# One layer of a hybrid attention step on one core: a measured cost model for the order of instructions, jobs on the divided array issued together, and a scan at the end of a search

## The chip, the cores and the metric

One NeuronCore of a Trainium2 chip runs the kernel. The time is device microseconds of one execution; the median of three runs is given. One further execution was recorded by the hardware profiler, and its rows are the ones quoted. Engines: PE is TensorE, PEld its weight loads, DVE is VectorE, ACT is ScalarE, POOL is GpSimd, SP issues the DMAs.

## The reference, cut to what matters

One layer step is computed for a prompt of 512 tokens and a sample of 32 tokens, each of width 1024. The sample has caches of 1024 past positions (the newest 512 of them for group A).

```
z = rmsnorm(x) @ w_in          # 1024 x 3880: q, k, v, gate of A, B; q, gate of M; indexer
A: 6 heads x 64, own chunk of 64 and 8 chunks before, learned relative bias
B: 6 heads x 64, rotary; an indexer of 8 heads x 32 gives
   score(q, s) = sum_h w_h relu(qi_h . ki_s);  the k best keys per query are attended
   (k = 128 for the prompt's 512 keys, 256 for the sample's 1024 + 32)
M: 4 heads x 64 over 256 memory tokens, k and v from rmsnorm(mem) @ w_mem_kv
x = x + concat(oA*silu(gA), oB*silu(gB), oM*silu(gM)) @ w_out
y = rmsnorm(x)                 # and the new keys and values are outputs too
```

Top k takes the lower position first among equal scores, which is why the search of the sample's choice has an end for ties.

## The kernel before, in words

All weights come from memory as 32-bit floats. ACT rounds each block to a short form (`wh`), POOL or DVE subtracts to get the rest (`wl`), and the activations are split in the same way (`xTh`, `xTl`, `oAh`, `oAl`). A projection is then three matmuls for each block of 128 inputs: `wh` by `xTh`, `wh` by `xTl`, `wl` by `xTh`. These make up most of PE's work. The projections run in the order of two lists, `EARLY` (A, M) and `LATE` (gate, k, q, v of B); then comes the output projection in chunks of columns, first for A and M (weights times `oA`, `oM`, `oS`), then for B (`oB`). `oS` is the sample's part.

Everything else is a task: a Python generator that issues some instructions and yields a time at which it wants to go on. Such tasks are the indexer (`index`), the prompt's picks with MAX and MATCH_REPLACE on `ysel`, the search of the sample's choice (`sample_choice`), the attention units (`attend`), the sample's attention (`sample`), and the evictions of banks (`evict`). A unit is one pair of heads with one tile of 128 queries or two: score matmuls (`u.begin`, named k,q in the rows), then DVE and ACT make `z` by mask, exp, sum and scaling, PE transposes `z` (ident,z), and `u.mix` multiplies with v (pt,vb). The result `o` is gated on DVE while it leaves its bank.

The order is set while the program is written. The class `Line` keeps a clock for each engine; each recorded instruction advances it by `cost`, and `lag` is what a result needs from one engine to another. The stream of projections is fill: before each of its steps `run` lets all tasks go on whose time has come by the model's clock. So a change of `cost` moves instructions on all engines. All instructions are issued through one helper, `Timed`, which is why every row of the profile names the same line.

PE can be divided with `tile_position`: products with only 64 or 32 rows or columns then run side by side on parts of the array. The sample's raw projection (`raw`, `xF`), scores and mixes of units and the sample's scores and mixes do so. `room` waits for a free bank of the eight.

The sample's choice is a search over bits of a threshold for 256 of 1056 keys for each of the 32 queries, four candidates at a time on 128 partitions. A pass is one Sign of 1056 on ACT with its sum, a Sign of the sum (`bf_ok`), a matmul of one column (bf_ok,over) that counts, and small operations on DVE. Before, a second search of six such passes over `rank` (positions among the equal scores) ended it.

At the end each tile of 128 rows gets its second half of 512 columns from PE; `residual` adds x on DVE, `settle` squares it with a sum on ACT, adds and takes the power on POOL (`ss`), and scales the second half on DVE and the first on ACT before the store.

Of the kernel before, what the change touches and what calls it, by code (L numbers as in the profile page):

```python
# [36 lines left out]
SURE = 1.0  # L37
LAG = 0.2
# [6 lines left out]
class Line:  # L45
# [4 lines left out]
    def __init__(self):  # L50
        self.clk = dict.fromkeys(("PE", "DVE", "ACT", "POOL", "SP", "DMA"), 0.0)
        self.ready, self.used = {}, {}
        self.boxes = {}
        self.tables = {"exp": (AF.Exp, AF.Tanh)}
        self.table = None
        self.tasks = []
        self.seq = 0
        self.margin = 0.3
        self.time = 0.0
        self.window, self.busy, self.slow = 0.0, 0.0, True  # L60
        self.warm = None

    def cost(self, eng, op, outs, ins, kw):
        if eng == "PE":
            w = 1 if ins[0].dtype in (F32R, BF16) else 2 if op == "transpose" else 4
            n = outs[0].free_size() * w / 2400.0
            if op == "matmul" and ins[0].dtype == F32R:
                return 0.003 + max(n, 0.104) if "tile_position" not in kw else 0.02 + 0.5 * max(n, 0.104)
            if "tile_position" in kw:
                return 0.04 + n * (0.25 if outs[0].shape[0] == T else 0.5)  # L70
            return 0.003 + n
        n = max(x.free_size() for x in outs[:1] + ins[:1])
        chip = ins and ins[0].space != PSUM
        if eng == "DVE":
            if op == "tensor_scalar" and chip and outs[0].dtype == F32 and "accum_out" not in kw:
                return 0.13 + n / 1920.0
            return (0.13 if op == "scalar_tensor_tensor" and chip else 0.07) + n / 960.0
        if eng == "ACT":
            t = 0.05 + 0.045 * bool(chip) + n / 1200.0 + (0.19 if "accum_out" in kw else 0)
            for table, fs in self.tables.items():  # L80
                if kw.get("func") in fs and self.table != table:
                    self.table = table
                    t += 1.3
            return t
        return 0.15 + n * (0.0034 if op == "tensor_scalar" else 0.0021)
# [56 lines left out]

    def op(self, eng, op, outs, ins, kw):
# [126 lines left out]
def hybrid_step(ctx: ExitStack, tc: tile.TileContext, a: dict):  # L270
# [37 lines left out]

    def take(k):
# [146 lines left out]
    def w_sample():  # L456
        for nm, i, n in parties:
# [3 lines left out]
            yield from room()  # L461
            p = bank()
            for j in (0, 2):
                for q in range(4):
                    PE.matmul(p[q * T:(q + 1) * T, 0:n], xF[:, 2 * j + q, :], raws[i + j + q // 2][:, q % 2, :],
                              start=(j == 0), stop=(j == 2), tile_position=(0, q * T))
# [3 lines left out]
    def sample_rows(nm, n, p):  # L470
# [15 lines left out]
        yield from line.wait(lambda: NT in normed)  # L486
# [451 lines left out]
    bf = {n: cp.tile([P, 1], F32, name="bf_" + n) for n in ("sum", "t", "c", "m", "need", "cut", "try", "dig", "min")}  # L938
# [3 lines left out]
    def sample_choice():  # L942
        flp, neg, ok, dig, nxt = (bi[n] for n in ("flip", "neg", "ok", "dig", "next"))
        thr = bi["thr0"], bi["thr1"]
        s_, t, c, m, need, cut, tr_, digf, okf = (bf[n] for n in ("sum", "t", "c", "m", "need", "cut", "try", "dig", "ok"))
# [4 lines left out]
        V.tensor_copy(digf, dig)  # L950
# [5 lines left out]
        def passed(of, bias, least_, scale=1.0):  # L956
# [3 lines left out]
            A.activation(okf, s_, AF.Sign, bias=least_, scale=scale)  # L960
# [29 lines left out]
        yield from line.wait(lambda: count["scored"] >= len(TILES))  # L990
# [19 lines left out]
        V.tensor_scalar(need, c, -2.0, float(2 * TOPK_S - NKS) + 0.5, op0=ALU.mult, op1=ALU.add)  # L1010
        G.iota(rank, pattern=[[-1, NKS]], base=2048, channel_multiplier=0, allow_small_or_imprecise_dtypes=True)
        yield max(line.at(rank), line.idle(V))
        V.scalar_tensor_tensor(rank, ysS, t, rank, op0=ALU.is_equal, op1=ALU.mult)
        V.memset(cut, 2048.5)
        V.tensor_scalar(tr_, digf, 1024.0, cut, op0=ALU.mult, op1=ALU.subtract)
        for b in range(10, -1, -2):
            w = float(1 << b)
            p = yield from passed(rank, tr_, need, -1.0)
            V.tensor_scalar(m, p[:, 0:1], 0.5 * w, 1.5 * w, op0=ALU.mult, op1=ALU.add)
            give(p)  # L1020
            V.tensor_scalar(cut, m, -1.0, cut, op0=ALU.mult, op1=ALU.add)
            if b:
                V.tensor_scalar(tr_, digf, 0.25 * w, cut, op0=ALU.mult, op1=ALU.subtract)
# [3 lines left out]
        V.scalar_tensor_tensor(ysS, rank, cut, ysS, op0=ALU.is_le, op1=ALU.mult)  # L1027
# [103 lines left out]
    def sample(mix, nh, nb, kt, cv, qT, kn, vn, pts, zin):  # L1131
# [18 lines left out]
        for g0 in range(0, nh, 4):  # L1150
# [9 lines left out]
            yield from room(len(cuts))  # L1160
            scs = [bank() for _ in cuts]
            for sc, (k0, n) in zip(scs, cuts):
                for j, h in enumerate(hs):
                    r = 64 * (h % 2)
                    PE.matmul(sc[T * j:T * j + T, 0:n], qT[r:r + 64, h // 2, -T:], kt[h // 2][r:r + 64, k0:k0 + n], start=True, stop=True,
                              tile_position=(r, T * j))
# [42 lines left out]
            for j0 in range(0, len(hs), 2):  # L1209
                for pt, b, i, w in blocks:  # L1210
                    for j in (j0, j0 + 1):
                        h = hs[j]
                        e = h % 2
                        vv = cv[b // 4][:, b % 4, h * 64:h * 64 + 64] if b < nb else vn[:, h * 64:h * 64 + 64]
                        PE.matmul(o_ps[64 * e:64 * e + 64, (h // 2) * T:(h // 2 + 1) * T], vv,
                                  pt[:, i * rows + T * j:i * rows + T * j + T], start=(b == 0),
                                  stop=(b * P + w == nk), tile_position=(0, 64 * e))
# [143 lines left out]
    class Masked:  # L1361
# [74 lines left out]
        def mix(self, pts, o):  # L1436
            for i, (t, c, n) in enumerate(self.parts):
                for b in range(n // P):
                    for e in range(2):
# [3 lines left out]
                                  tile_position=(0, 64 * e))  # L1443

# [21 lines left out]
    def attend(i):  # L1466
# [10 lines left out]
        yield from room(2)  # L1477
        sc = u.begin()
# [11 lines left out]
        yield from room()  # L1490
        o = bank()
        u.mix(pts, o)
# [46 lines left out]
    line.until(lambda: 1 in gated and all(n in over for n in ("kb", "qb", "vb")))  # L1539
# [38 lines left out]
    def out_part(parts, c0, n, done, order):  # L1578

        ws = [w_next(1 + i) for i in range(len(parts))]  # L1580
        for t in order:
            acc, = take(1)
            for i, ((m, k0, nk, p0, pn), (wh, wl)) in enumerate(zip(parts, ws)):
                o = acc[:, p0:p0 + pn]
# [15 lines left out]
            line.spawn(evict([acc], [1], lambda _, p, t=t: residual(t, p, c0, n), lambda t=t: done(t)))  # L1600
# [6 lines left out]
    for c0 in range(0, D, 256):  # L1607
        line.run(out_part(((0, 0, 3, 0, 256), (2, 6, 2, 0, 256)), c0, 256, lambda t: None, (0, 1, 2, 3, NT)))
# [10 lines left out]
    def settle(t, c0):  # L1619
        rows = P if t < NT else T  # L1620
        x = xr[t][:, c0:c0 + 512]
        s_ = ss[:rows, t, :]
        last = c0 + 512 == D
        yield line.at(x) - 0.2
        A.activation(sq[:rows], x, AF.Square, scale=D ** -0.5, accum_out=s_[:, c0 // 512:c0 // 512 + 1])
        if not last:
            G.tensor_tensor(x, x, gf[:rows, c0:c0 + 512], op=ALU.mult)
        yield line.at(s_) - 0.2
        if not last:
            V.tensor_scalar(s_[:, 2:3], s_[:, 0:1], EPS, None, op0=ALU.add)  # L1630
            return
        G.tensor_tensor(s_[:, 3:4], s_[:, 1:2], s_[:, 2:3], op=ALU.add)
        G.tensor_tensor(s_[:, 4:5], s_[:, 3:4], nhalf[:rows], op=ALU.pow)
        yield line.at(s_) - 0.2
        y = xr[t]
        V.scalar_tensor_tensor(x, x, s_[:, 4:5], gf[:rows, c0:D], op0=ALU.mult, op1=ALU.mult)
        A.activation(y[:, 0:512], y[:, 0:512], AF.Copy, scale=s_[:, 4:5])
        DMA.dma_start(a["y_prompt"][t * P:(t + 1) * P, :] if t < NT else a["y_sample"], y)

    for c0 in range(0, D, 512):  # L1640
        line.run(out_part(((1, 3, 3, 0, 256), (1, 3, 3, 256, 256)), c0, 512, lambda t, c0=c0: line.spawn(settle(t, c0)),
                          (NT, 0, 1, 2, 3)))
# [67 lines left out]
```

## Time and profile before

| | |
|---|---|
| median of 3 runs | 369.21 us (368.37 to 370.45) |
| profiled execution, its own time | 369.7 us |
| its span in the profile | 367.9 us |
| mean granted clock of PE | 0.992 |
| from the start of the span to the first wait's end on PE | 1.35 us |
| DMA | 46.35 MB, mean 126 GB/s |
| DVE, ACT, POOL busy | 282.4, 223.0, 176.2 us |

The profiled execution's time is 1.8 above its span, for what lies around the profiled instructions. A row of a timeline has start, length, engine, the program's line, operation, output and inputs, shapes and, in brackets, idle time before it with what ended it. Ends of matmuls are modelled and overlap; the distance of two starts is what one costs. Rows of the page's groups have the count, then busy us and mean ns.

### The profile page before, as it was taken

Reading aid. Unit: us, or ns where it says so; the run is one execution under the profiler, and the core shown is the slowest. Engines: PE = TensorE matmul, PEld = TensorE weight load, DVE = VectorE, ACT = ScalarE, POOL = GpSimd, SP = SyncE. Lnnn points to the kernel's source line nnn. Section 1 sums busy time; section 2 is a strip of 40 time slices with the busy share of each in tenths; the row PEclk is TensorE's granted clock in tenths of the full one; section 3 lists DMA queues with packets and bytes.
Section 4 is the critical chain, followed back from the end, with each engine's and each line's share of the span. In section 5 each row is a group of like instructions: output and inputs, shape, how many; then the busy total and the mean of one; then the engine's idle time right before and its main releaser. Section 6 shows DMA issues by size and latency. Waiting matters only on the chain.

```text
span 367.9 us, 7969 instructions
## 1 busy us (share of the span) xinstructions
PE 355.6 (97%) x2959; PEld 321.6 (87%) x2959; DVE 282.4 (77%) x731; ACT 223.0 (61%) x524; POOL 176.2 (48%) x202
## 2 busy tenths in 40 slices
PE   8999999999999999999999998999999999999992
PEld 8989679999989988889899787898999879899991
DVE  2682996989999999999999989986764676623553
ACT  5865756997776946788737343767864556311343
POOL 1787953475443834446548447352145206233651
PEclk9999999999999999999999998999999999999998
DMA  7996631366483330611322115121147932120005
GB/s 252 361 361 220 172 116 43 130 178 172 127 272 104 116 89 11 175 47 45 86 64 67 45 48 172 37 59 54 48 159 259 375 98 88 43 102 2 0 20 224
DMA packets 41478, 46.35 MB, mean 126 GB/s; under 512 B 5184, under 2 KB 36544, under 8 KB 41440
## 3 DMA queue, kind: packets, MB, share of 16 engines
q1 hardware_dynamic: 41440, 45.85, 39.2%
q8 instruction: 23, 0.38, 0.4%
q14 instruction: 15, 0.12, 0.1%
HBM read 39.67 MB, written 6.16 MB: 125 GB/s over the span
## 4 chain that ended last, share of the span: by engine, by line
PE 77%; DVE 11%; ACT 3%; POOL 3%; issue 2%; DMA 2%; SPq 1%; POOLq 0%; ACTq 0%; DVEq 0%
PE bank L240 77%; DMA raw<-in_w_in_dram 2%; DVE rt L240 1%; POOL wl L240 1%; DVE rank L240 1%; DVE KSs L240 1%; ACT sq L240 1%; DVE ysel L240 1%; DVE kb L240 1%; POOL ss L240 1%; DVE kbS L240 1%; DVE m L240 1%; SPq L240 1%; DVE bf_m L240 1%; POOL kb L240 1%
## 5 line engine op out<-in xcount | busy, mean ns | idle before, releaser
L240 POOL TENSOR_TENSOR wl<-raw,wh 128x512 fp32r<-128x512 f32 (+2 forms) x68 | 105.1, 1553 | 95.6 <-ACT wh L240 91.8
L240 PE MATMUL bank<-wh,xTh 128*128 128x384 f32 (+1 forms) x192 | 67.5, 351 | 0.1
L240 ACT ACTIVATE wh<-raw 128x512 fp32r<-128x512 f32 (+2 forms) x70 | 49.8, 717 | 28.4 <-issue 11.8
L240 PE MATMUL bank<-wl,xTh 128*128 128x384 f32 (+1 forms) x192 | 64.0, 334 | 0.2 <-DVE wl L240 0.2
L240 PE MATMUL bank<-wh,xTl 128*128 128x384 f32 (+1 forms) x192 | 63.7, 332 | 0.0
L240 ACT ACTIVATE z<-z,st 128x256 f32<-128x256 f32 (+3 forms) x76 | 40.6, 549 | 35.1 <-DVE st L240 35.0
L240 PE MATMUL bank<-xTh,wh 128*128 128x272 f32 x208 | 46.3, 304 | 0.3 <-DVE stS L240 0.3
L240 PE MATMUL bank<-xTh,wl 128*128 128x272 f32 x208 | 43.0, 288 | 0.0
L240 PE MATMUL bank<-xTl,wh 128*128 128x272 f32 x208 | 43.0, 288 | 0.0
L240 PEld LDWEIGHTS bank<-wh,xTh 128*128 128x128 f32 x192 | 36.6, 191 | 3.9 <-issue 2.6
L240 PEld LDWEIGHTS bank<-wl,xTh 128*128 128x128 f32 x192 | 36.5, 190 | 0.6 <-DVE wl L240 0.4
L240 PEld LDWEIGHTS bank<-wh,xTl 128*128 128x128 f32 x192 | 36.8, 191 | 0.3 <-DVE xTl L240 0.3
L240 PEld LDWEIGHTS bank<-xTh,wh 128*128 128x128 f32 x208 | 32.7, 189 | 3.1 <-issue 2.0
L240 PEld LDWEIGHTS bank<-xTl,wh 128*128 128x128 f32 x208 | 32.6, 188 | 0.0
L240 PEld LDWEIGHTS bank<-xTh,wl 128*128 128x128 f32 x208 | 32.5, 189 | 0.0
L240 DVE MAX8 m<-ysel 128x8 f32<-128x256 f32 (+2 forms) x48 | 26.4, 550 | 0.1
L240 DVE MATCH_REPLACE8 ysel<-m,ysel 128x256 f32<-128x256 f32 (+2 forms) x48 | 26.0, 542 | 0.0
L240 PE MATMUL bank<-ident,z 128*128 128x128 f32 (+1 forms) x161 | 25.2, 274 | 0.5 <-ACT z L240 0.4
L240 DVE TENSOR_TENSOR xr<-bank,xr 128x256 f32<-128x256 f32 (+1 forms) x24 | 12.2, 510 | 16.7 <-PE bank L240 15.6
L240 PEld LDWEIGHTS bank<-ident,z 128*128 128x128 f32 (+1 forms) x161 | 18.3, 140 | 3.6 <-issue 1.4
L240 DVE SCALAR_TENSOR_TENSOR ysel<-r,wI,ysel 128x256 f32<-128x256 f32 (+2 forms) x21 | 18.5, 880 | 3.0 <-ACT r L240 2.5
L240 ACT ACTIVATE junkS<-ysS,bi_neg 128x1056 int8<-128x1056 f32 x16 | 18.7, 1172 | 2.3 <-DVE bi_neg L240 2.3
(317 smaller groups left out, 884.1 us busy)
## 6 DMA issues: line engine op xcount, KB each, us to landing
raw<-in_w_in_dram SPq DMA_DIRECT2D x20, 384.0 KB, 3.3
raw<-in_w_in_dram SPq DMA_DIRECT2D x26, 256.0 KB, 2.9
raw<-in_w_out_dram SPq DMA_DIRECT2D x8, 384.0 KB, 3.0
nat<-in_x_prompt_dram SPq DMA_DIRECT2D x4, 512.0 KB, 8.2
raw<-in_w_mem_kv_dram SPq DMA_DIRECT2D x8, 256.0 KB, 2.9
xr<-in_x_prompt_dram SPq DMA_DIRECT2D x4, 512.0 KB, 5.3
out_dram<-xr SPq DMA_DIRECT2D x4, 512.0 KB, 2.6
xr<-in_x_t_dram SPq DMA_DIRECT2D x3, 544.0 KB, 5.9
```

Of the source, the lines that this page charges most:

```text
L240: return fn(*args, **kw)
```

## The change

Four things are changed together.

1. `Line.cost` for PE is a table of measured figures instead of a formula, with an extra for a change between the forms of the divided array (`mode`). All other engines' costs are multiplied by `SLACK` = 1.3. A DMA is taken to need 1.6 us and then to move 330 GB/s, instead of 1.1 us and 360. `port` keeps DVE and POOL apart in the model for operations that `shares` names.
2. `divided` takes jobs for the divided array. A job waits for up to `HOLD` = 3 us of the model's time until a second one is there; all that have banks are then issued in one go. The sample's raw projections, the units' scores and mixes and the sample's scores and mixes go through it.
3. The six tie passes at the end of `sample_choice` are replaced by an equality test, a scan over 1056 columns that counts the equal ones, and a comparison. This end, and the scaling by `rs` and the rotation of the sample's `kb` and `qb`, start only when "qb" is done.
4. In the last chunk of the output, the last tile (`NT-1`) is evicted in two pieces of 256 columns, and the first half of the tile before it is scaled on DVE instead of ACT.

```diff
+SLACK = 1.3
+HOLD = 3.0
...
         if eng == "PE":
-            w = 1 if ins[0].dtype in (F32R, BF16) else 2 if op == "transpose" else 4
-            n = outs[0].free_size() * w / 2400.0
-            if op == "matmul" and ins[0].dtype == F32R:
-                return 0.003 + max(n, 0.104) if "tile_position" not in kw else 0.02 + 0.5 * max(n, 0.104)
...
+            if op == "transpose":
+                d = max(0.085 if fast else 0.109 * ins[0].shape[0] / P, 0.06)
+            elif fast:
+                d = max(n / 2400.0 + 0.013, 0.107 if n > 1 else 0.04)
+            else:
+                d = 2 * max(n / 1190.0, 0.058)
...
+            if mode != self.mode:
+                self.mode = mode
+                d += 0.095 + (0.104 if fast else 0.056) * mode[1] / P
+            return d
...
-            t = max(t + 1.1, self.clk["DMA"])
-            end = t + outs[0].size() * 4 / 360e3
+            t = max(t + 1.6, self.clk["DMA"])
+            end = t + outs[0].size() * 4 / 330e3
...
-            d = self.cost(eng, op, outs, ins, kw)
+            d = self.cost(eng, op, outs, ins, kw) * (1.0 if eng == "PE" else SLACK)
             if eng == "PE":
                 d = self.array(t, d)
+            elif eng == "POOL" or eng == "DVE" and self.shares(op, outs, ins):
+                t = self.port(eng, t, d)
...
+    def divided(k, issue):
+
+        if k:
+            yield from room(k)
+        job = [k, issue, None, False]
+        waiting.append(job)
+        end = line.now() + HOLD
+        while not job[3]:
+            if len(waiting) == 1 and line.now() < end:
+                yield min(end, line.soon())
+                continue
+            if not there(k):
+                yield from room(k)
+                continue
+            for j in [job] + [j for j in waiting if j is not job]:
+                if there(j[0]):
+                    waiting.remove(j)
+                    j[2], j[3] = j[1](), True
+        return job[2]
...
-        yield from line.wait(lambda: NT in normed)
+        yield from line.wait(lambda: NT in normed and (nm not in ("kb", "qb") or "qb" in over))
...
-        for b in range(10, -1, -2):
-            w = float(1 << b)
-            p = yield from passed(rank, tr_, need, -1.0)
...
+        V.tensor_scalar(junkS, ysS, t, None, op0=ALU.is_equal)
+        yield line.idle(V)
+        V.tensor_tensor_scan(rank, junkS, junkS, 0.0, op0=ALU.add, op1=ALU.max)
+        yield line.idle(V)
+        V.scalar_tensor_tensor(rank, rank, need, junkS, op0=ALU.is_lt, op1=ALU.mult)
...
-        yield from room(2)
-        sc = u.begin()
+        sc = yield from divided(2, u.begin)
...
-        yield from room()
-        o = bank()
-        u.mix(pts, o)
+        o = yield from divided(1, lambda: u.mix(pts, bank()))
...
+                if i and t in apart:
+                    line.spawn(evict([acc], [1], lambda _, p, t=t: residual(t, p[:, 0:p0], c0, p0),
+                                     lambda t=t: done(t, c0, p0)))
+                    acc, = take(1)
...
-        A.activation(y[:, 0:512], y[:, 0:512], AF.Copy, scale=s_[:, 4:5])
+        if t == NT - 2:
+
+            V.tensor_scalar(y[:rows, 0:512], y[:rows, 0:512], run, None, op0=ALU.mult)
+        else:
+            A.activation(y[:rows, 0:512], y[:rows, 0:512], AF.Copy, scale=run)
```

Three places show how instructions move. The first is DVE around the second score of a unit of M, during the projections of `kb` and `qb` (`rt` and `kb` are the rotation's products on their way out of the banks, `o` frees the bank of a finished unit). Before:

```order
L240 TENSOR_TENSOR rt<-bank,sin_122 128x384
L240 TENSOR_TENSOR kb<-bank,cos_120 128x384
L240 MAX m_75<-ysel_73 128x8
L240 MATCH_REPLACE ysel_73<-m_75,ysel_73 128x512
L240 TENSOR_TENSOR rt<-bank,sin_122 128x384
L240 TENSOR_TENSOR kb<-bank,cos_120 128x384
L240 TENSOR_TENSOR rt<-bank,sin_122 128x384
L240 TENSOR_TENSOR kb<-bank,cos_120 128x384
L240 TENSOR_TENSOR kb<-rt,kb 128x384
L240 TENSOR_TENSOR qbS<-bank,qbS 32x384
L240 SCALAR_TENSOR_TENSOR o<-bank,gate 128x256
```

The same stretch of DVE after:

```order
L273 SCALAR_TENSOR_TENSOR o<-bank,gate 128x128
L273 MAX m_75<-ysel_73 128x8
L273 MATCH_REPLACE ysel_73<-m_75,ysel_73 128x512
L273 RECIPROCAL st<-st 128x4
L273 TENSOR_SCALAR z<-z,st 128x256 x2
L273 TENSOR_TENSOR rt<-bank,sin_122 128x384
L273 TENSOR_TENSOR kb<-bank,cos_120 128x384
L273 TENSOR_TENSOR rt<-bank,sin_122 128x384
L273 TENSOR_TENSOR kb<-bank,cos_120 128x384
L273 TENSOR_REDUCE st<-bank 128x2 x2
L273 MAX m_75<-ysel_73 128x8
L273 MATCH_REPLACE ysel_73<-m_75,ysel_73 128x512
```

`o` of the unit before now stands ahead of the pairs of `rt` and `kb`, and the reductions of a unit of M (its scores are on PE by then) stand directly behind two of them.

The second place is PE at the end of B's attention in the prompt. Before, with the sample's transposes behind the last mix and output projections on both sides:

```order
L240 MATMUL bank<-wh,oAl 128x256
L240 MATMUL bank<-wl,oAh 128x256
L240 MATMUL bank<-pt,vb 64x128 x8
L240 MATMUL bank<-ident,z_3919 128x64 x8
L240 MATMUL bank<-ident,z_3919 32x64
L240 MATMUL bank<-wh,oMh 128x256
L240 MATMUL bank<-wh,oMl 128x256
L240 MATMUL bank<-wl,oMh 128x256
```

After, on PE:

```order
L273 MATMUL bank<-wl,oMh 128x256
L273 MATMUL bank<-ident,z 128x128 x3
L273 MATMUL bank<-wh,oS 64x256
L273 MATMUL bank<-wl,oS 64x256
L273 MATMUL bank<-wh,oS 64x256
L273 MATMUL bank<-wl,oS 64x256
L273 MATMUL bank<-ident,z 128x128 x4
L273 MATMUL bank<-pt,vb 64x128 x6
L273 MATMUL bank<-ident,z 128x128 x4
L273 MATMUL bank<-pt,vb 64x128 x14
L273 MATMUL bank<-wh,oS 64x256
L273 MATMUL bank<-wl,oS 64x256
```

The mixes have moved to the end of the first part of the output projection: the last two sets of transposes have only six mix matmuls between them, and what follows is the sample's part of the output of B.

The third place is the end of DVE's program (`xr_` with a number is a tile of 128 rows; the last number is the last tile). Before:

```order
L240 TENSOR_TENSOR xr_3895<-bank,xr_3895 128x512
L240 SCALAR_TENSOR_TENSOR xr_3894<-xr_3894,ss,gf 128x512
L240 TENSOR_TENSOR xr_3896<-bank,xr_3896 128x512
L240 SCALAR_TENSOR_TENSOR xr_3895<-xr_3895,ss,gf 128x512
L240 SCALAR_TENSOR_TENSOR xr_3896<-xr_3896,ss,gf 128x512
```

After, on DVE:

```order
L273 TENSOR_TENSOR xr_3719<-bank,xr_3719 128x512
L273 SCALAR_TENSOR_TENSOR xr_3718<-xr_3718,ss,gf 128x512
L273 TENSOR_TENSOR xr_3720<-bank,xr_3720 128x256 x2
L273 SCALAR_TENSOR_TENSOR xr_3719<-xr_3719,ss,gf 128x512
L273 TENSOR_SCALAR xr_3719<-xr_3719,ss 128x512
L273 TENSOR_SCALAR ss<-ss 128x1
L273 SCALAR_TENSOR_TENSOR xr_3720<-xr_3720,ss,gf 128x512
```

The last tile's add is in two halves, and the scaling of the first half of the tile before it and the small sum of the last tile now stand between them and the last product.

More of the change, by code (lines that the diff above doesn't have):

```diff
@@ L55, in __init__ @@
         self.table = None
+        self.mode = None
+        self.taken = []
         self.tasks = []
@@ L141, in array, with shares, port @@
         return d
+    @staticmethod
+    def shares(op, outs, ins):
+        if outs[0].space == PSUM or any(x.space == PSUM for x in ins):
+            return False
+        full = [x for x in ins if x.free_size() > 1]
+        if op in ("scalar_tensor_tensor", "tensor_tensor"):
+            return True
+        return op in ("tensor_scalar", "tensor_copy") and len(full) > 0 and outs[0].dtype == F32
+    def port(self, eng, t, d):
+        for s, end, by in self.taken:
+            if by != eng and s <= t < end:
+                t = end
+        self.taken = [x for x in self.taken[-40:]] + [(t, t + d, eng)]
+        return t
     def op(self, eng, op, outs, ins, kw):
@@ L307, in room, with there @@
             yield from line.wait(lambda: len(free_banks) >= k)
+    waiting = []
+    def there(k):
+        return k == 0 or len(free_banks) >= k and sorted(pp.free(f"b{b}") for b in free_banks)[k - 1] + 0.4 <= line.now()
+    def divided(k, issue):
[16 more added lines that the diff above has]
+        return job[2]
     def take(k):
@@ L460, in w_sample, with issue @@
             yield line.sure(xF, *raws[i:i + 4])
-            yield from room()
[L462 to L466, printed above, removed]
+            def issue():
+                p = bank()
+                for j in (0, 2):
+                    for q in range(4):
+                        PE.matmul(p[q * T:(q + 1) * T, 0:n], xF[:, 2 * j + q, :], raws[i + j + q // 2][:, q % 2, :],
+                                  start=(j == 0), stop=(j == 2), tile_position=(0, q * T))
+                return p
+            p = yield from divided(1, issue)
             met.extend(range(i, i + 4))
@@ L989, in sample_choice @@
                 V.tensor_scalar(neg, dig, b - 2, old, op0=ALU.logical_shift_left, op1=ALU.bitwise_xor)
-        yield from line.wait(lambda: count["scored"] >= len(TILES))
+        yield from line.wait(lambda: count["scored"] >= len(TILES) and "qb" in over)
         rank = cp.tile([P, NKS], F32, tag="rank", name="rank")
@@ L1159, in sample, with scores_of @@
             cuts = [(k0, min(512, nk - k0)) for k0 in range(0, nk, 512)]
[L1160 to L1166, printed above, removed]
+            def scores_of():
+                scs = [bank() for _ in cuts]
+                for sc, (k0, n) in zip(scs, cuts):
+                    for j, h in enumerate(hs):
+                        r = 64 * (h % 2)
+                        PE.matmul(sc[T * j:T * j + T, 0:n], qT[r:r + 64, h // 2, -T:], kt[h // 2][r:r + 64, k0:k0 + n],
+                                  start=True, stop=True, tile_position=(r, T * j))
+                return scs
+            scs = yield from divided(len(cuts), scores_of)
             for sc, (k0, n) in zip(scs, cuts):
@@ L1208, in sample, with mix_of @@
             yield line.sure(*cv)
[L1209 to L1217, printed above, removed]
+            def mix_of():
+                for j0 in range(0, len(hs), 2):
+                    for pt, b, i, w in blocks:
+                        for j in (j0, j0 + 1):
+                            h = hs[j]
+                            e = h % 2
+                            vv = cv[b // 4][:, b % 4, h * 64:h * 64 + 64] if b < nb else vn[:, h * 64:h * 64 + 64]
+                            PE.matmul(o_ps[64 * e:64 * e + 64, (h // 2) * T:(h // 2 + 1) * T], vv,
+                                      pt[:, i * rows + T * j:i * rows + T * j + T], start=(b == 0),
+                                      stop=(b * P + w == nk), tile_position=(0, 64 * e))
+            yield from divided(0, mix_of)
         yield from line.wait(lambda: mix in gated)
@@ L1538, in hybrid_step @@
     projections(LATE)
-    line.until(lambda: 1 in gated and all(n in over for n in ("kb", "qb", "vb")))
+    line.until(lambda: 1 in gated and all(n in over and n in news for n in ("kb", "qb", "vb")))
     rox.close()
@@ L1576, in hybrid_step, with out_part @@
     line.spawn(sample_b())
-    def out_part(parts, c0, n, done, order):
+    def out_part(parts, c0, n, done, order, apart=()):
         ws = [w_next(1 + i) for i in range(len(parts))]
@@ L1617, in hybrid_step, with settle @@
     ss = fp.tile([P, NT + 1, 8], F32, name="ss")
-    def settle(t, c0):
+    pieces = [0] * (NT + 1)
+    def settle(t, c0, n):
         rows = P if t < NT else T
-        x = xr[t][:, c0:c0 + 512]
+        x = xr[t][:, c0:c0 + n]
         s_ = ss[:rows, t, :]
-        last = c0 + 512 == D
+        j = pieces[t]
+        pieces[t] += 1
+        new, run, old = s_[:, 2 * j:2 * j + 1], s_[:, 2 * j + 1:2 * j + 2], s_[:, 2 * j - 1:2 * j]
         yield line.at(x) - 0.2
[L1625 to L1630, printed above, removed]
+        A.activation(sq[:rows, 0:n], x, AF.Square, scale=D ** -0.5, accum_out=new)
+        if j == 0:
+            G.tensor_tensor(x, x, gf[:rows, c0:c0 + n], op=ALU.mult)
+        yield line.at(new) - 0.2
+        if c0 + n < D:
+            V.tensor_scalar(run, new, EPS if j == 0 else old, None, op0=ALU.add)
```

49 lines of the change are left out of this document (21 added, 28 removed).

## The prediction

> **What bounds the kernel now.** I read the page's busy times first, then what TensorE waited for, then busy time by stretch, and only then single instructions.
>
> ```profile
> PE 355.6 (97%) x2959; PEld 321.6 (87%) x2959; DVE 282.4 (77%) x731; ACT 223.0 (61%) x524; POOL 176.2 (48%) x202
> ```
>
> TensorE is busy for 97% of the span, so the time is its work, plus its few gaps, plus the tail after its last matmul. No other engine is close to being the bound over the whole. The gaps, by what ended them:
>
> ```profile
> PE bank L240 <- POOL nhalf L240: 1.4, 1, 1.4
> PE bank L240 <- DVE o L240: 1.3, 1, 1.3
> PE bank L240 <- DVE stk L240: 0.7, 2, 0.4
> PE bank L240 <- ACT z L240: 0.4, 1, 0.4
> PE bank L240 <- DVE stS L240: 0.3, 1, 0.3
> PE bank L240 <- DVE KSs L240: 0.2, 1, 0.2
> PE bank L240 <- DVE wl L240: 0.2, 1, 0.2
> PE bank L240 <- DVE kl L240: 0.2, 1, 0.2
> ```
>
> Columns: who waited for whom, us in all, times, the longest. The first row is the start of the program, which the edit leaves alone. The others make 3.3 us; that is all an order of the same work can win, plus what a gap costs afterwards. The stretches show that this second part exists (columns: stretch, length, busy us of PE, PEld, DVE, ACT, POOL, then granted clock, DMA share, GB/s):
>
> ```profile
> 222.00:224.00 2.00, 0.86 (x5) 0.41 (x3) 1.94 (x3) 0.00 (x0) 2.00 (x2) 1.00 0.00 0
> 226.00:228.50 2.50, 2.50 (x9) 2.35 (x8) 2.40 (x6) 1.56 (x3) 1.24 (x1) 0.50 1.03 330
> 323.50:341.80 18.30, 18.30 (x157) 18.26 (x155) 5.57 (x14) 2.99 (x5) 6.76 (x5) 1.00 0.15 52
> ```
>
> PE is busy for 0.86 of 2 us at 222, and two microseconds later its clock is granted at 0.50 for a while. The third row is the stretch after the last sparse attention unit: pure output projection, PE full, DVE at 5.57 of 18.30. That is spare cover the old order leaves unused, and the new order spends it.
>
> **The change, part by part.** Sum against the profiled execution, 369.7 us, which lies 0.5 above the median of the runs, 369.21.
>
> *The stall at 222.* Here are DVE and POOL, then PE at that place:
>
> ```profile
> 220.82 3.93 POOL L240 TENSOR_TENSOR wl<-raw,wh 128x768 fp32r<-128x768 f32 x2
> 221.25 1.83 DVE L240 TENSOR_TENSOR kb<-rt,kb 128x384 f32<-128x384 f32 x1
> 223.11 0.55 DVE L240 TENSOR_TENSOR qbS<-bank,qbS 32x384 f32<-32x384 f32 x1
> 223.69 0.42 DVE L240 SCALAR_TENSOR_TENSOR o<-bank,gate 128x256 f32<-128x256 f32 x1
> 222.48 0.38 PE L240 MATMUL bank<-k,q 64*128 64x256 f32 x1
> 224.17 0.38 PE L240 MATMUL bank<-k,q 64*128 64x256 f32 x1 [1.31 <-DVE o L240]
> 225.08 0.44 PE L240 MATMUL bank<-wh,xTh 128*128 128x384 f32 x1
> 228.79 0.48 PE L240 MATMUL bank<-k,q 64*128 64x256 f32 x2
> 229.79 0.44 PE L240 MATMUL bank<-wh,xTh 128*128 128x384 f32 x1
> 231.82 0.34 PE L240 MATMUL bank<-wl,xTh 128*128 128x384 f32 x1
> ```
>
> The second score matmul needs the bank that DVE's `o` empties. `o` stands behind `kb` and `qbS`, and `kb` ran 1.83 us while POOL worked on two splits of 1.96 each. The group of scores from 222.48 to 225.08 took 2.60, the same group from 228.79 to 229.79 took 1.00: 1.60 lost. The twelve matmuls from 225.08 to 228.79 took 3.71; the same twelve from 229.79 end, by the last start at 231.82 and the spacing of 0.18, at 232.0, so 2.2: 1.5 lost to the half clock. Together 3.1. In the new order of DVE (front of this document) the four `rt`/`kb` pairs no longer stand in one piece before `o`; between them are the reductions and the scaling of a unit whose scores were thus already issued, and the sample's `kb`/`qb` scaling and rotation were moved behind "qb". POOL's splits stay as long as they were. I take the whole 3.1 as gone; bounds 0 (the same collision with another instruction) and −3.1.
>
> *Head, 36 to 51 us.* PE waits here for stacks that DVE builds late:
>
> ```profile
> 39.92 2.05 DVE L240 TENSOR_TENSOR stk<-rotS,stk 32x512 fp32r<-32x512 f32 x1 [0.69 <-ACT stk L240]
> 41.90 3.05 DVE L240 TENSOR_SCALAR wsel<-ident,wS 32x128 f32<-32x128 f32 x8
> ```
>
> The waits for `stk` and `KSs` sum to 0.9. New order: the prompt's stacks are ahead of the sample's on DVE, so some of it goes. What is late next is the sample's own `stk`, which PE needs after 50 us. I take −0.8 with the short restarts behind each wait, bounds 0 and −1.5 (0.9 plus about 0.2 for each of three restarts, an estimate from the 0.44 against 0.34 of a first matmul in the rows at 225 and 231).
>
> *Waits for `z` and `kl`, and for `stS`.* In the list 0.4, 0.2 and 0.3. In the new order of PE the transposes of `z` stand further behind the scores they come from, and the sample scores are issued when two jobs are ready. −0.8 for `z` and `kl` with their restarts, −0.5 for `stS`; bounds 0 and −1.6 together.
>
> *Holding jobs on the divided array, and fewer small matmuls.* The cost of going from the full to a divided array and back can be read from two blocks of six equal matmuls, the first between transposes on the full array, the second ahead of scores on the divided one:
>
> ```profile
> 262.99 0.42 PE L240 MATMUL bank<-wh,xTh 128*128 128x384 f32 x1
> 264.13 0.60 PE L240 MATMUL bank<-ident,z 128*128 128x128 f32 x4
> 264.48 0.42 PE L240 MATMUL bank<-wh,xTh 128*128 128x384 f32 x1
> 265.71 0.33 PE L240 MATMUL bank<-k,q 64*128 64x128 f32 x2
> L240 PE MATMUL bank<-bf_ok,over 128*128 128x1 bf16 x22 | 3.9, 176 | 0.0
> ```
>
> 1.14 against 1.23: 0.09 for a change of form. Counted in the two orders, PE changes its form 125 times before and 129 times after, so the hold saves none: +4 x 0.09 = +0.4. The Trainium skill, "TensorEngine Tiling (Array Packing)", Tiling Modes, speaks for what the hold is after: "Changing tiling mode (not just tile) drains the TensorE". By that rule the part pays only where the count of changes falls; here it rises by four, which turns the rule against it. Six of 22 `bf_ok` matmuls go with the tie passes. Their 0.176 is overlapped; I count 0.05 each, −0.3, bounds 0 and −1.1. The new end of the search costs nothing on PE: DVE loses the six rounds of small operations and one 1056-wide pass, gains an equality test and a scan. No row shows a scan. Net PE work: +0.1, bounds −0.7 and +0.4.
>
> *The end of sparse attention.* Before, its last transposes and mixes on PE lie ahead of 323.5, where the 18.3 us of cover shown above begin. After, the last three units come about 20 us later: the order ends `ident,z` x4, `pt,vb` x6, `ident,z` x4, `pt,vb` x14, and the output of B follows at once. What a unit needs between its scores and its transposes (mask, exp, sum, scaling on DVE and ACT) is at most this, from a place without a wait:
>
> ```profile
> 285.48 0.40 PE L240 MATMUL bank<-kl,q 64*128 64x512 f32 x2
> 290.83 0.66 PE L240 MATMUL bank<-ident,z 128*128 128x128 f32 x4
> ```
>
> 5.35 us. Adding the spacings of the matmuls that stand between in the new order gives 7.4 us for the last unit and at least 7.9 for all others, so it is covered by 2.0 us. DVE has eviction adds in its queue there, and a collision as at 221 lengthens one operation by 1.3 (1.83 against 0.55 of the 32-row form at 223.11, of the same width). I take +0.5; bounds 0 and +4.
>
> *The tail.* Chain after the last matmul, which ends at 360.62:
>
> ```profile
> 360.34 0.28 PE L240 MATMUL bank<-wl,oBh 128*128 128x256 f32 x1
> 360.65 0.69 DVE L240 TENSOR_TENSOR xr<-bank,xr 128x512 f32<-128x512 f32 x1 [0.81 <-PE bank L240]
> 361.20 0.72 ACT L240 ACTIVATE xr<-xr,ss 128x512 f32<-128x512 f32 x1 [0.94 <-POOL ss L240]
> 361.26 0.74 DVE L240 SCALAR_TENSOR_TENSOR xr<-xr,ss,gf 128x512 f32<-128x512 f32 x1
> 361.83 0.61 ACT L240 ACTIVATE sq<-xr 128x512 f32<-128x512 f32 x1
> 362.61 0.19 POOL L240 TENSOR_TENSOR ss<-ss 128x1 f32<-128x1 f32 x1 [1.45 <-ACT sq L240]
> 363.46 0.75 DVE L240 SCALAR_TENSOR_TENSOR xr<-xr,ss,gf 128x512 f32<-128x512 f32 x1 [1.46 <-POOL ss L240]
> ```
>
> Before: 364.21, 3.59 after the end of PE, and then the last store. The edit takes the 0.72 of ACT off the way of the square and halves the add and the square. But DVE's queue now reads: scaled product of tile 2, then its first half (new on DVE), then the small sum of tile 3, and only behind it POOL's two steps. From the end of PE: the product from +0.64 to +1.38, the half to about +2.0 (0.6, an estimate below the 0.75 of the two-operand form), the small sum to +2.15, POOL's steps as before 0.85, some 0.1 of handing over, the product 0.75: +3.85. So +0.2; bounds −0.9 (if the queue did not matter: 0.4 for the halved add, 0.6 for the halved square, then 0.95 and 0.75) and +0.5.
>
> *What no row shows.* A new order of some 2,600 matmuls makes waits of its own. Without the 1.3 at 222 the old one has 2.0 of them; I take half of that, +1.0, bounds 0 and +3.
>
> Sum: −3.1 −0.8 −0.8 −0.5 +0.1 +0.5 +0.2 +1.0 = −3.4, so 366.3 profiled and 365.8 against the median.
>
> **Rivals.** *Stalls only move.* The waits are about seven in 358 us of work; the order comes from a model of clocks, not from the trace, and the DMAs and splits on POOL are untouched. If the gaps and one half-clock stretch come back elsewhere, the gain terms (5.2) are eaten and 369.0 to 369.7 is left. For it: POOL's wide splits still meet DVE. Against: the distances on PE are longer at every place named.
>
> *Slower: the end of sparse attention is not covered.* The point from which it decides is a chain of the last unit above 7.4. One collision gives 5.35 + 1.3 = 6.7, still covered; two, or one with two eviction adds of 0.7 ahead in the queue, give some 8, and nothing else is left to fill. A wait of over 1.3 at 222 brought 1.5 of half clock, so a chain of 10 to 11 costs 3 to 4 and with that 1.5, at three units perhaps more: 365.8 + 5 to 6 = 371 to 372. The Trainium skill, "SBUF — State Buffer", states that DVE and GpSimd hold their shared port as an exclusive lock for a whole instruction; by that rule each meeting can add a POOL instruction's whole length, 1.96 by the row at 220.82, which makes the two-collision case 9.3 and this rival likelier. The row at 221.25 (DVE done only after the first split) agrees.
>
> *The hold and the new end do nothing.* Order's gains at zero but also no new wait: by the form changes, +0.4, and the tail, +0.2, less 0.3: 369.5. For it: the count of changes did not fall.
>
> **How the numbers follow.** Forecast 0.58, stalls move 0.20, uncovered end 0.17, nothing 0.05. A measurement of this kernel can tell about 0.5% (1.85 us) from no change. All the forecast's cases lie below 367.4 but for some 0.01 that end at the same; of the uncovered end 0.15 lie above 371.1, the rest within. With 0.02 of the moved stalls on the slow side: faster 0.57, same 0.26, slower 0.17. The range: at the low end all gains at their bounds without new waits (−3.1 −1.5 −1.6 −0.3: 362.7 against the median), at the high end the uncovered end with one short wait and no half clock, 370.5. The forecast's own range is 363.5 to 367.3.
>
> **What the changed profile would show.** Right: no wait over 0.5 in PE's list behind the start, the granted clock at 1.0 in all slices from 20 to 355 us, PE's last matmul near 357, and 3.6 to 3.9 us from it to DVE's last product. Wrong: a wait of PE for ACT or DVE `z` around 335 to 340 us of over 1 us with a clock of 0.5 behind it; a new PE wait around 205 to 235; or PE's busy time over 356.5, which would say that the divided array costs more than the 0.09.

## The result and the profile after

The changed kernel takes 363.29 us (median of 4 runs, 362.68 to 363.68), beside 369.66 for the kernel before (4 runs, 368.37 to 370.45). The ratio is 0.9833, 95% interval 0.981 to 0.9856: 1.7% faster, 6.4 us between the medians. It lies inside the predicted range of 362.7 to 370.5, close to its lower end, and 0.2 below the forecast's own 363.5 to 367.3; the predicted 365.8 took little over half of the gain. Single executions over 1.5% above the fastest of their kernel (389.19 us with HOLD = 0, 387.23 with SLACK = 1.4 and 1513.33 of before, in the experiments below) are left out of medians and ranges.

The page of the changed kernel, span and busy times, then what PE waited for over the whole span:

```profile
span 360.6 us, 7941 instructions
...
PE 350.7 (97%) x2961; PEld 320.0 (89%) x2961; DVE 276.6 (77%) x696; ACT 219.6 (61%) x521; POOL 191.0 (53%) x213
```
```profile
PE bank L273 <- POOL nhalf L273: 1.4, 1, 1.4
PE bank L273 <- ACT pt L273: 0.7, 2, 0.4
```

Of 3.3 us of waits behind the start 0.7 is left, in two places. The two windows that were worst before (same columns as in the prediction, after) show PE full and its clock at 1.00; the kernel computes something else there now, so it is the whole list above that says that the stall did not move:

```profile
222.00:224.00 2.00, 2.00 (x22) 1.16 (x21) 1.84 (x3) 0.00 (x0) 2.00 (x2) 1.00 0.00 0
226.00:228.50 2.50, 2.50 (x18) 2.46 (x17) 2.44 (x5) 0.93 (x2) 1.10 (x3) 1.00 0.39 114
```

The two waits, and the end of sparse attention, on PE's timeline:

```profile
179.44 0.16 PE L273 MATMUL bank<-bf_ok,over 128*128 128x1 bf16 x1 [0.34 <-ACT pt L273]
...
265.03 1.09 PE L273 MATMUL bank<-pt,mv 128*64 128x128 f32 x14 [0.37 <-ACT pt L273]
...
322.53 0.40 PE L273 MATMUL bank<-kl,q 64*128 64x512 f32 x2
...
331.13 0.66 PE L273 MATMUL bank<-ident,z 128*128 128x128 f32 x4
331.72 1.94 PE L273 MATMUL bank<-pt,vb 128*64 128x128 f32 x28
333.59 0.33 PE L273 MATMUL bank<-wh,oS 128*64 128x256 f32 x1
```

The last unit has 8.6 us from its last scores to its last transposes, and no bracket stands at them: the cover was enough. The tail, all engines:

```profile
352.58 0.28 PE L273 MATMUL bank<-wl,oBh 128*128 128x256 f32 x1
...
352.89 0.42 DVE L273 TENSOR_TENSOR xr<-bank,xr 128x256 f32<-128x256 f32 x1 [0.17 <-PE bank L273]
...
353.54 0.42 ACT L273 ACTIVATE sq<-xr 128x256 f32<-128x256 f32 x1
...
353.90 0.75 DVE L273 SCALAR_TENSOR_TENSOR xr<-xr,ss,gf 128x512 f32<-128x512 f32 x1 [0.59 <-POOL ss L273]
354.57 0.48 DVE L273 TENSOR_SCALAR xr<-xr,ss 128x512 f32<-128x512 f32 x1
354.97 0.21 DVE L273 TENSOR_SCALAR ss<-ss 128x1 f32<-128x1 f32 x1
355.32 0.19 POOL L273 TENSOR_TENSOR ss<-ss 128x1 f32<-128x1 f32 x1 [1.45 <-DVE ss L273]
355.59 0.55 POOL L273 TENSOR_TENSOR ss<-ss,nhalf 128x1 f32<-128x1 f32 x1
...
356.17 0.75 DVE L273 SCALAR_TENSOR_TENSOR xr<-xr,ss,gf 128x512 f32<-128x512 f32 x1 [1.00 <-POOL ss L273]
```

PE ends at 352.86 (360.62 before), and the last product at 356.92: 4.06 behind it, beside 3.59 before. So PE's end came 7.8 us earlier, and 0.5 of it was given back behind PE. Summing the distances of PE's starts in the two traces, by kind, gives where the 7.8 came from: gaps of over 0.2 in the streams of projection matmuls 4.43 to 0.21 (−4.2); the rest that a stall leaves in them (half clock, small gaps) 5.15 to 3.85 (−1.3); the matmuls' own distance, −2.3; the first matmul after an interruption, 109 of them before and 104 after, −0.5; all other work on PE +0.6. That last figure holds the wait at 222, which lies between two score matmuls: the scores with their waits fall by 1.35, and the transposes of `z` and the mixes of M take 0.8 more each, 0.7 of that in the two new waits.

### The profile page after: what moved, and what is told of

It is laid out like the page before. It is cut to its first block, busy times and chain, and to the rows that moved or that the text cites. A ratio compares the mean times of both kernels' runs of the same rounds, so it can differ in the third digit from the quotient of the medians.

```text
span 360.6 us, 7941 instructions
## 1 busy us (share of the span) xinstructions
PE 350.7 (97%) x2961; PEld 320.0 (89%) x2961; DVE 276.6 (77%) x696; ACT 219.6 (61%) x521; POOL 191.0 (53%) x213
## 4 chain that ended last, share of the span: by engine, by line
PE 89%; DVE 4%; DMA 2%; issue 1%; ACT 1%; POOL 1%; SPq 1%; POOLq 0%; ACTq 0%; DVEq 0%
PE bank L273 89%; DMA raw<-in_w_in_dram 2%; POOL ss L273 1%; DVE ysel L273 1%; ACT sq L273 1%; DVE xr L273 1%; SPq L273 1%; DVE z L273 1%; DVE m L273 0%; DVE xTl L273 0%; DVE gate L273 0%; ACT wh L273 0%; ACT xTh L273 0%; DVE o L273 0%; DVE pt L273 0%
## 5 line engine op out<-in xcount | busy, mean ns | idle before, releaser
L273 POOL TENSOR_TENSOR wl<-raw,wh 128x512 fp32r<-128x512 f32 (+2 forms) x68 | 110.0, 1622 | 78.2 <-ACT wh L273 74.4
L273 ACT ACTIVATE wh<-raw 128x512 fp32r<-128x512 f32 (+2 forms) x70 | 50.1, 719 | 33.1 <-issue 13.6
L273 PE MATMUL bank<-wh,xTh 128*128 128x384 f32 (+1 forms) x192 | 65.3, 340 | 0.0
L273 ACT COPY pt<-bank 128x512 f32<-128x512 f32 (+1 forms) x26 | 14.1, 543 | 14.3 <-PE bank L273 14.2
L273 POOL TENSOR_TENSOR oBl<-o,oBh 128x128 fp32r<-128x128 f32 (+1 forms) x9 | 4.9, 549 | 30.4 <-ACT oBh L273 30.4
```

What stands on the lines that cost most here:

```text
L273: return fn(*args, **kw)
```

## The experiments

**Is the stall at 222 the same in every execution?** The kernel before, profiled a second time.

> The kernel before, a second profile. Theory 1 (everything comes from the change of order): the output projection's matmuls of 256 columns start 0.120 us apart as in the first profile, the stall at 222 us is there again with a wait of 1.2 to 1.4 us, span 367 to 369 us. Theory 3 (part of the gain is a state of the execution and not of the kernel): the distances are 0.113 in all or part of the output projection, or the stall at 222 has another length, and the span differs by over 1 us from 367.9.

It took 368.87 us in this execution. PE's list has the wait again, but the window behind it has the full clock:

```profile
PE bank L240 <- DVE o L240: 1.3, 1, 1.3
```
```profile
222.00:224.00 2.00, 1.32 (x7) 0.88 (x5) 1.97 (x2) 0.00 (x0) 2.00 (x2) 1.00 0.00 0
226.00:228.50 2.50, 2.50 (x21) 2.25 (x21) 2.29 (x7) 1.57 (x3) 1.71 (x1) 1.00 1.02 295
```

The wait belongs to the kernel. The half clock behind it came in one execution and not in the other, at 0.5 us of difference in when the group of scores began (222.48 and 222.95); why is not shown. Of the 3.1 that the prediction put on this place, 1.5 is paid in some executions only, and so is the −1.3 in the sum above: what a stall leaves in the streams is 3.87 here, beside 5.15 in the first profile and 3.85 after the change. By its numbers theory 1 holds (a wait of 1.3, a span of 367.1, distances in the output projection of 0.120 again); the clock stood in neither theory.

**Each part alone on the kernel before.** First the model, `Line.cost`, reserve, DMA and port (the diffs of these three runs are given in short):

```diff
+ cost() by measured figures and mode; SLACK = 1.3; DMA 1.6 us and 330 GB/s; port()
  room(2); sc = u.begin()      # no hold
  old end of the search, old tail
```

> Before with the new model of costs alone (PE's table, the reserve of 1.3, the DMA's figures, the shared port). Theory 1 (the order's model carries the gain): 363 to 365 us, PE's list of waits under 1.5 us behind the start, no slice with a low clock. Theory 2 (the new end of the search and its postponement clear the place at 222 us and carry the gain): 367 to 370, the waits of 205 to 235 still there.

376.31 us (374.21 to 376.68), ratio 1.0174 (1.0124 to 1.0224): slower by 7, against both theories. PE's list has 9.2 us of waits beside 3.3; the largest five, in three groups:

```profile
PE bank L273 <- DVE pt L273: 2.9, 1, 2.9
PE bank L273 <- ACT bf_ok L273: 2.4, 2, 2.0
PE bank L273 <- DVE kb L273: 2.0, 2, 1.7
```

Then the hold alone, with the old model:

```diff
+ HOLD = 3.0; divided(k, issue) for raw, scores and mixes
  cost(), DMA, no SLACK, old search, old tail
```

> Before with the hold alone (jobs on the divided array wait up to 3 us for each other; changes of form counted 126 instead of 125). The theory that holding saves changes of form: 1 us or more faster, 366 to 368. The prediction's count: no change in PE's work, 368.5 to 370.5, with the order's waits moved at random.

385.86 us (384.45 to 387.23), ratio 1.045 (1.0406 to 1.0493): 17 us slower, against both expectations. 17 waits, the largest:

```profile
PE bank L242 <- ACT bf_ok L242: 3.6, 4, 1.5
PE bank L242 <- DVE st L242: 3.2, 3, 2.2
PE bank L242 <- DVE o L242: 2.1, 2, 1.4
```

And the new end of the search alone:

```diff
- six passes of Sign, bf_ok and a matmul over rank
+ is_equal; tensor_tensor_scan; is_lt; wait for "qb"
  old model, no hold, old tail
```

> Before with the new end of the search alone (equality test, scan, postponed behind qb, and the sample's kb and qb scaled later). Theory 1: 368 to 370 us, since the order elsewhere is the old one and its waits stay or move. Theory 2: 365 to 367, the 3.1 us of the stall at 222 and its half clock are gone and nothing takes their place.

368.21 us (367.53 to 368.96), ratio 0.9976 (0.9958 to 0.9994). The wait for `o` at 222 is gone from the list, and two others, of 2.0 and 0.5, are new. The longer one, at 252 us, is where the sparse units now meet the search on DVE:

```profile
PE bank L240 <- DVE ql L240: 2.5, 2, 2.0
```

Theory 1 holds for the time, and theory 2 falls: clearing that one place is worth nothing if the same operations come down on the next. Nor need this small gain be the search's own: the distance of 256-column matmuls was 0.113 here, and the next two runs price that at about 1 us.

**Why the matmuls of the output projection are closer together.** In every kernel above with the old search those with `oB` start 0.120 apart, in every one with the new search 0.113. The new search has two one-column tiles less. In the built programs that moves the weight blocks 64 bytes down in each partition: their addresses are 96 modulo 128 before and 32 after. They are the moving operand; `oA`, `oB` and `oM`, which are loaded as the next weights meanwhile, are at 96 in both. (The tiles of `raw`, `xTh` and `xTl` move with the weight blocks.) Two kernels move them and leave the order of every engine as it was:

```diff
# after
- ("sum", "t", "c", "m", "need", "try", "min")
+ ("sum", "t", "c", "m", "need", "try", "min", "pad0", "pad1")
```

> After with two unused tiles of one column added, so that the weight blocks lie 64 bytes further in each partition; the order of every engine is the same. Theory of the address (a 256-column matmul takes 0.120 when its moving operand and the weights loaded for the next one lie at the same address modulo 128 bytes, 0.113 when they lie 64 bytes apart): the output projection goes back to 0.120, and the kernel takes 1.5 to 2.5 us more, 365 to 366. Theory that the distance belongs to the order or to the state of PE's queue: 0.113 stays, 363.3 within 0.5.

```diff
# before: "need", "dig" and "min" as columns of one tile
+ bf3 = cp.tile([P, 3], F32, name="bf_three")
```

> Before with three one-column tiles of the search laid into one tile of three columns, so that the weight blocks lie 64 bytes lower; the order is the same. Theory of the address: 0.113 in the output projection, 1.5 to 2.5 us less than before, 366.5 to 368. Theory of the order: 0.120 and no difference.

After with the two tiles back: 364.38 us (364.25 to 364.46), 1.1 above after. Before with 64 bytes less: 367.89 (366.6 to 368.78), ratio 0.9963 (0.9948 to 0.9978), 1.2 below before. Starts in the output projection, first of after with the tiles, then of before without them:

```profile
347.02 0.28 PE L273 MATMUL bank<-wh,oBh 128*128 128x256 f32 x1
347.14 0.28 PE L273 MATMUL bank<-wh,oBl 128*128 128x256 f32 x1
347.26 0.28 PE L273 MATMUL bank<-wl,oBh 128*128 128x256 f32 x1
```
```profile
347.04 0.28 PE L240 MATMUL bank<-wl,oBh 128*128 128x256 f32 x1
347.15 0.28 PE L240 MATMUL bank<-wh,oBh 128*128 128x256 f32 x1
347.26 0.28 PE L240 MATMUL bank<-wh,oBl 128*128 128x256 f32 x1
```

The distances change places with the address, at the same order. The medians move by less than the expected 1.5 to 2.5. Matched one by one, the matmuls of the output projection take 2.0 us more in the first and 2.2 less in the second; those of the memory projection go the other way, by 0.35 and 0.2, which leaves +1.6 and −2.1 with small differences elsewhere. Other gaps add 0.7 in both traces. Before with 64 bytes less also ran more often at a lower clock: the five of its twelve executions with a mean clock of 0.993 or more took 366.60 to 367.43, beside 368.11 to 369.56 in 18 of 22 of before, so at equal clock the gain is about 2.0.

**The hold, taken away and shortened.**

```diff
- HOLD = 3.0
+ HOLD = 0.0        # the first run;  2.0 in the second
```

> After with HOLD = 0: jobs on the divided array no longer wait for each other (128 changes of form instead of 129). Theory that the hold does nothing and that the model with its reserve, the search's new end and the address carry the gain: 362 to 365 us. Theory that the parts only work together (the model alone lost 7 us): 367 us or more, with PE waits of over 3 us.

370.5 us (369.65 to 372.55), ratio 1.005 (1.0029 to 1.007), 7.2 above after and within what the second theory expected. One place makes most of it, where a prompt unit and the sample's memory attention meet on DVE and ACT (the wait, then windows with the clock in the third column from the end):

```profile
PE bank L273 <- DVE pt L273: 2.8, 1, 2.8
```
```profile
174.00:178.00 4.00, 1.16 (x17) 0.91 (x14) 3.90 (x9) 3.83 (x11) 2.53 (x5) 1.00 0.00 0
178.00:182.00 4.00, 4.00 (x22) 4.00 (x21) 3.58 (x9) 2.19 (x6) 3.10 (x3) 0.57 0.00 0
```

> After with HOLD = 2 us of the model's time instead of 3. Theory that holding itself helps, smoothly in its length: between 363 and 366. Theory of one lucky order: anywhere from 363 to 376, as HOLD = 0 was at 370.6, with one or two single stalls that make up the whole difference to after.

365.25 us (364.78 to 366.81), ratio 0.9895 (0.9863 to 0.9927). Waits of 3.5 in eight places, none over 0.7: no single stall makes up the difference, and the time falls with the length of the hold at these three values, as the first theory has it. It is not shown that the hold does this by itself, since each value also gives another order, and on the kernel before the hold cost 17 us. Changes of form explain little: there are 128, 128 and 129 at 0, 2 and 3 us, and counted between the full array and any other form 116, 108 and 108, of which eight at 0.09 would be 0.7.

**The reserve, smaller and larger.**

```diff
- SLACK = 1.3
+ SLACK = 1.0       # the first run;  1.4 in the second
```

> After with the reserve SLACK at 1.0 instead of 1.3. Theory that the reserve turns off the waits (the model then places work on PE before ACT, DVE and POOL have finished): PE waits behind the start of over 3 us, most of them for ACT or DVE z and pt, and 366 to 370 us. Theory that the measured costs do it alone: under 1.5 us of waits and 362 to 364.5.

383.89 us (383.74 to 384.2), ratio 1.0404 (1.038 to 1.0428): far beyond what the theory of the reserve expected. The largest of 17 waits:

```profile
PE bank L273 <- ACT z L273: 2.8, 1, 2.8
PE bank L273 <- DVE z L273: 2.4, 3, 1.3
PE bank L273 <- POOL rs L273: 2.1, 1, 2.1
```

> After with SLACK = 1.4. Theory of the reserve (enough of it turns off waits, more costs little): PE waits behind the start under 2.5 us, 362.5 to 365.5. Theory of one lucky order (each model gives some order, and 1.3 with HOLD = 3 was picked because it came out well): 367 us or more, single waits of 2 us and more with a half clock behind them.

382.7 us (381.4 to 383.62), ratio 1.0343 (1.0299 to 1.0386). More reserve is as bad as none, so the theory of the reserve falls. The largest of 12 waits, and the window of one of them:

```profile
PE bank L273 <- ACT z L273: 3.5, 1, 3.5
PE bank L273 <- DVE z L273: 3.5, 3, 3.0
PE bank L273 <- DVE QS L273: 3.0, 1, 3.0
```
```profile
262.00:275.00 13.00, 8.93 (x67) 7.28 (x66) 12.89 (x21) 9.15 (x28) 10.22 (x9) 0.74 0.47 169
```

Seen together, PE's waits behind the start (sum of the list, profiled execution) and the median times go nearly in one order, whatever the kernel's parts. Below 6 us of waits the order is not strict, and there the address counts too (the last column has the distance of the matmuls with `oB`):

| kernel | PE's waits, us | longest | time, us | distance |
|---|---|---|---|---|
| after | 0.7 | 0.4 | 363.29 | 0.113 |
| after, two tiles more | 1.2 | 0.5 | 364.4 | 0.120 |
| HOLD = 2 | 3.5 | 0.7 | 365.25 | 0.113 |
| before | 3.3 | 1.3 | 369.1 | 0.120 |
| search alone | 5.1 | 2.0 | 368.2 | 0.113 |
| before, 64 bytes less | 5.4 | 1.3 | 367.9 | 0.113 |
| HOLD = 0 | 5.8 | 2.8 | 370.5 | 0.113 |
| model alone | 9.2 | 2.9 | 376.3 | 0.120 |
| SLACK = 1.4 | 13.4 | 3.5 | 382.7 | 0.113 |
| SLACK = 1.0 | 13.6 | 2.8 | 383.9 | 0.113 |
| hold alone | 16.1 | 2.2 | 385.9 | 0.120 |

From after to the hold alone that is 22.6 us of time for 15.4 us of waits, 1.5 for 1; the other rows with the distance of 0.113 and over 5.5 us of waits give 1.4 to 1.6.

**The tail.** Two changes to the end of after; PE's order is the same in both.

```diff
-            V.tensor_scalar(run, new, EPS if j == 0 else old, None, op0=ALU.add)
+            (the sum with old on POOL: G.tensor_tensor(run, new, old, op=ALU.add))
```

> After with the small sum of the last tile on POOL instead of DVE, so that it no longer stands behind tile 2's two products in DVE's queue. Reading of the tail by DVE's queue: the last product ends 1.0 us earlier, 3.1 after the end of PE instead of 4.06, and the kernel takes 0.8 to 1.0 less, about 362.4. Reading by the power on POOL or by the last store: no difference beyond 0.3.

362.84 us (362.77 to 363.78), ratio to before 0.9828 (0.9803 to 0.9852). Its range overlaps that of after, so the 0.45 between the medians is not clear of noise. In the trace the last product ends 3.39 behind PE, 0.7 earlier than in after; the expected 1.0 was not reached, since POOL's two steps now lie beside DVE's operations and take 0.51 and 0.68 instead of 0.19 and 0.55:

```profile
353.20 0.28 PE L273 MATMUL bank<-wl,oBh 128*128 128x256 f32 x1
...
354.81 0.51 POOL L273 TENSOR_TENSOR ss<-ss 128x1 f32<-128x1 f32 x1 [0.16 <-ACT sq L273]
...
355.41 0.68 POOL L273 TENSOR_TENSOR ss<-ss,nhalf 128x1 f32<-128x1 f32 x1
356.12 0.75 DVE L273 SCALAR_TENSOR_TENSOR xr<-xr,ss,gf 128x512 f32<-128x512 f32 x1 [0.44 <-POOL ss L273]
```

```diff
- apart=(NT - 1,) ; V.tensor_scalar for tile NT - 2
+ one piece of 512 ; A.activation for every tile
```

> After with the tail of before (last tile evicted in one piece of 512, first half of tile 2 scaled on ACT); PE's order is the same. By the traces (4.06 after, 3.59 before) the edit of the tail loses: 362.7 to 363.0, last product 3.6 after PE. If the edit helps: 363.8 or more.

362.4 us (362.23 to 362.66), ratio to before 0.9812 (0.9789 to 0.9834), the fastest of all; its five runs lie below all four of after, 0.9 between the medians. So the edit of the tail loses, and by more than the 0.3 to 0.6 expected. The last product ends 3.26 behind PE, not 3.6:

```profile
353.07 0.28 PE L273 MATMUL bank<-wl,oBh 128*128 128x256 f32 x1
...
354.17 0.63 ACT L273 ACTIVATE sq<-xr 128x512 f32<-128x512 f32 x1 [0.71 <-DVE xr L273]
354.80 0.70 ACT L273 ACTIVATE xr<-xr,ss 128x512 f32<-128x512 f32 x1
...
355.86 0.75 DVE L273 SCALAR_TENSOR_TENSOR xr<-xr,ss,gf 128x512 f32<-128x512 f32 x1 [0.72 <-POOL ss L273]
```

ACT now squares tile 3 ahead of copying tile 2; in the kernel before it was the other way round. What the edit of the tail wanted to take off the path, the new order alone had already taken off.

## Why the prediction was right, and where its terms were off

- *The stall at 222, −3.1.* Gone, as forecast (−1.7 and −1.4 against the usual distances in the profiled execution). That the search's part is enough to clear it is shown by the search alone; the wider spacing was not tried apart. That clearing it is a gain is not shown, since there a wait came back at 252 us; and the 1.4 of half clock is paid in some executions only.
- *Head, −0.8.* Its bound of −1.5 was reached: no block of PE between 40 and 51 us has over 0.1 too much in after.
- *`z`, `kl` and `stS`, −1.3.* All three waits are gone, −1.6 with their restarts.
- *PE's work, +0.1 within −0.7 and +0.4.* This is the term that failed. I counted instructions and changes of form and took the distance of matmuls as fixed; it fell by 6% for the 256 columns of the output projection, because the search's smaller tiles moved the weight blocks. By the distances −2.3, by the medians −1.1 to −1.2, outside the bounds I gave. The +0.4 for changes of form has no measurement behind it: both traces change 108 times between the full array and another form, which is what the 0.09 prices, and the four more are changes among the other forms. The drain that the Trainium skill, "TensorEngine Tiling (Array Packing)", Tiling Modes, tells of would lie within that 0.09. No run here separates it.
- *End of sparse attention, +0.5.* Four blocks there have 0.1 to 0.2 too much, together 0.6. The rival of an uncovered end did not come: 8.6 us of cover where I had counted 7.4, and no wait at its transposes.
- *Tail, +0.2.* +0.5: the order of DVE's queue was read rightly, and my sum of 3.85 (0.26 above before) came out at 4.06. The product of tile 2 began 1.04 behind PE's end, not 0.64, since it waited for POOL's `ss`; the first half took 0.48 where I had put 0.6.
- *New waits, +1.0.* Two waits of 0.7 in all, 1.7 with what stands around them at 179 and 264 us.
- *The sum.* These come to −5.7, beside 7.3 in the span. The rest lies in places that the prediction did not price, gaps of 0.37 and 0.23 at 7 and 76 us among them, and is not attributed in full. Without the address the kernel takes 364.38, inside the forecast's own range: the mechanism forecast (an order with few waits) gives most of the gain, and the address came on top unforeseen. PE's last matmul ends at 352.9, where the prediction's signs had 357.
- *The range.* Its low end of 362.7 is said to have all gains at their bounds, but it leaves out the −0.9 of the tail and takes −0.3 of PE's −0.7; with these it is 361.4. And by the prediction's own terms the rival of moving stalls comes to 370.0, not to 369.0 to 369.7.
- *Stalls only move* was the rival nearest to what the neighbours do. Of the six other settings of model, hold and reserve four are slower than before by 1.7% or more, one is slower by 0.5%, and only HOLD = 2 is faster. The prediction read the new order at the places of the old waits; that it makes so few of its own was not worked out but put in as +1.0, and is in part luck. It did not see how narrow the good place is, and 0.17 for slower is small beside these neighbours.

Left open: whether the hold and the reserve have an effect of their own, apart from the one order that they lead to. Six settings say that the time follows the waits. Along the hold the waits fall at 0, 2 and 3 us; along the reserve 1.3 lies between two values that lose 20 us. That the values 1.3 and 3 were picked for their result is likely and not shown.

## What to carry to other kernels

Where a host-side model sets the order of thousands of instructions, a change of the model or of one part is a new draw of the order, worth −2 to +5% here; judge the order that comes out, by the waits of the bound engine, and expect no part to keep its gain without the others. A stall of the bound engine cost about one and a half times its length here: the one of 1.3 at 222 us cost 1.7, and 3.1 in the execution where the clock fell behind it. Compare matmul distances between two kernels before trusting that the same work costs the same: an unrelated small tile can shift operands into or out of a slower address.

## What the runs showed of the hardware that was not expected

A matmul of 256 columns in the three-product stream took 0.120 from start to start when the moving operand and the weights loaded next lay at the same address modulo 128 bytes (96 and 96), and 0.113 at 32 and 96; the memory projection showed the same (0.119 at 32 and 32, 0.114 to 0.117 at 96 and 32). The sample's rows, with weights of 64 columns, showed the opposite (0.114 at 32 and 32, 0.117 at 96 and 32), so the residue is a mark and not the whole cause. The projections of 272 and 384 columns have both operands at one residue in every kernel, 96 or 32, and keep their 0.125 and 0.175; they do not test it. The scan, for which the prediction had no row, took more than any other pass of its width on DVE or ACT:

```profile
L273 DVE TENSOR_TENSOR_SCAN rank<-junkS 128x1056 f32<-128x1056 int8 x1 | 2.3, 2345 | 0.0
L273 DVE SCALAR_TENSOR_TENSOR rank<-rank,bf_need,junkS 128x1056 f32<-128x1056 f32 x1 | 1.3, 1325 | 0.0
```

A wait of PE of 1.3 us was followed by the half clock in one execution (a granted clock of 0.50 from 226 to 228.5 us) and not in another of the same program (1.00); before with 64 bytes less, in the same order, had it again (0.58).
